# w_out with tokens on the partitions, norms by rows, and u of the next round loaded in the middle of a round

## The chip, the cores and the metric

The kernel runs on one core of a Trainium2 chip. The time is the device time of one execution in microseconds (us). Engines: PE multiplies matrices, ACT (scalar), DVE (vector) and POOL do elementwise work, SP issues most DMAs. All five take their instructions in order.

## The reference

One layer of a hybrid decoder over 1024 prompt tokens and 8 x 4 decode tokens (1056 rows, width 1024). The stages up to the merged gates stay as they are; the change is in what follows them:

```python
def rmsnorm(x, g):
    r = lax.rsqrt(jnp.mean(xf * xf, axis=-1, keepdims=True) + RMS_EPS)
    return (xf * r).astype(x.dtype) * g
...
y = (jax.nn.sigmoid(ga) * ya + jax.nn.sigmoid(gb) * yb) @ w_out      # 1024 -> 1024
x = x + gt_m * rmsnorm(y, g_post_mix)
h2 = rmsnorm(x, g_pre_mlp) * (1 + sc_f) + sh_f
u = jnp.square(jax.nn.relu(h2 @ w_up))                               # 1024 -> 4096
x = x + gt_f * rmsnorm(u @ w_down, g_post_mlp)                       # 4096 -> 1024
```

`gt_m`, `sc_f`, `sh_f`, `gt_f` are vectors of 1024 that depend on the sequence (one for the prompt, eight for the decode rows). All is float32.

## The kernel before

**Precision.** A float32 product is three fp32r matmuls per block of 128 rows of the contraction: with each operand split into a rounded part h and the remainder l, they are h·h, h·l and l·h. So each operand needs a cast (ACT) and a difference (DVE or POOL). For weights this is `split4` (L1234 to L1241): a cast of 128x512 (L1238) and a difference (L1240) that goes to POOL, and every third time to DVE.

**Stages.** Times are from the span's start. `merge_b` (L1197) ends at 1011; its result m, split, lies in R0 to R7, channels on the partitions, in four chunks of 264 tokens.

1. *w_out* (1017 to 1129). Weights stationary, m moving: for each of 8 blocks of 128 output channels and each chunk 24 matmuls of 264 columns (L1458 to L1460), tokens in two halves of 528 one after the other: 768 matmuls. y comes out with channels on the partitions, as the residual x must then lie: 80 transposes turn x (L1334).
2. *Norms* (`norms`, L1352). With channels on the partitions, a sum over channels is a matmul by ones (L1266), and 1/rms is spread over the partitions by another (L1279). Between them stand scalings (L1344), adds (L1366), squares and sums (L1371, L1372), one block of 528 columns at a time.
3. *Operands* (`operands`, L1393). Strassen's scheme for `w_up` works on 2x2 blocks of h2 and of the weights: seven products instead of eight. The sums of blocks of h2 (L1405 to L1408) are split as well (L1312, L1313).
4. *plain* (1129 to 1220). While half 1 still goes through norms and operands, the first six column pairs of `w_up` are multiplied with half 0 by the ordinary scheme: 576 matmuls of 264 columns (L1513 to L1515).
5. *pair* (L1520; 1220 to 1505). Ten column pairs with both halves and the six with half 1 alone, by Strassen: 2184 matmuls of 264 columns (L1489 to L1491). The weights' block sums S (L1530 to L1533) and the results' adds (L1547) are on DVE. u goes to memory (L1502).
6. *Down* (1495 to 1913). Eight rounds of 512 rows of `w_down`, each 288 matmuls of 352 columns (L409 to L411). `load_u` (L1585) brings u of a round back and splits it: four casts (L1594), four differences (L1595) in turn on POOL and DVE. For round 0 it is called after two of the six half pairs and writes R0 to R3; for the others it is called at the round's start. The last round ends chunk by chunk with the norm, the residual and the output; x is turned back for it (L1658).

**What sets the order.** A scheduler places the instructions of each engine from the program's order and its own cost model; `tc.issue_after(ins)` and the tables `AT_OUT`, `XT_AT` and `AT_UP` say after which matmul a step of norms and operands is issued. Tiles have names and fixed numbers of buffers: a tile waits until the last reader of the buffer is done. DMAs of the queue SP are issued in order, and one that waits for a buffer holds back those behind it.

## Time and profile before

| | us |
|---|---|
| three runs | 1918.61, 1920.29 (median), 1930.76 |
| the profiled execution | 1914.69 |
| its span, first to last instruction | 1913.0 |
| PE busy | 1839.1 (96%) |
| DVE / ACT / POOL busy | 960.2 (50%) / 829.5 (43%) / 542.2 (28%) |
| mean granted clock | 0.976 of 2.4 GHz |

A matmul's busy time begins before the one ahead of it has ended, so a PE that is busy all the time need not be at its peak; the distance from one start to the next is what a matmul costs. The rows on which the prediction rests stand in a section below.

### The profile page before, as it was taken

What the parts mean: (1) busy time and instruction counts of PE and PEld (TensorE: products, weight loads), DVE (VectorE), ACT (ScalarE), POOL (GpSimd) and SP (SyncE); (2) the same over time, 40 slices, a digit from 0 to 9 for tenths busy, and PEclk for the clock granted to TensorE, in tenths of its full rate; (3) what the DMA queues carried; (4) which work ended last, traced back from release to release, by engine and by line L of the source; (5) the groups of instructions that cost most, each with busy time, mean ns of one, the idle gap of its engine ahead of it and who ended that gap; (6) DMA issues with size and microseconds to landing.
All of it is one profiled execution on the core that took longest, in us unless ns stands there. A gap on an engine that the chain in (4) does not pass through costs nothing.

```text
span 1913.0 us, 31223 instructions
## 1 busy us (share of the span) xinstructions
PE 1839.1 (96%) x12425; PEld 1733.9 (91%) x12425; DVE 960.2 (50%) x1904; ACT 829.5 (43%) x1513; POOL 542.2 (28%) x461
## 2 busy tenths in 40 slices
...
GB/s 272 78 69 60 148 92 68 56 79 111 174 168 220 70 62 58 77 201 111 67 97 156 123 99 161 94 107 119 90 134 148 122 135 90 90 90 90 90 55 128
DMA packets 180874, 213.29 MB, mean 111 GB/s; under 512 B 13940, under 2 KB 142512, under 8 KB 180728
## 3 DMA queue, kind: packets, MB, share of 16 engines
...
## 4 chain that ended last, share of the span: by engine, by line
PE 86%; DVE 5%; DMA 4%; issue 1%; ACT 1%; SPq 1%; POOL 1%; DVEq 0%; ACTq 0%; POOLq 0%
PE ps_g L409 17%; PE ps_g L411 17%; PE ps_g L410 17%; PE ps_s L685 2%; PE ps_g L1489 2%; PE ps_g L1491 2%; PE ps_g L1490 2%; PE ps_t L710 2%; PE ps_s L682 1%; PE ps_s L1491 1%; PE ps_s L1489 1%; PE ps_s L1490 1%; PE ps_t L1489 1%; PE ps_t L1490 1%; PE ps_t L1491 1%
## 5 line engine op out<-in xcount | busy, mean ns | idle before, releaser
L409 PE MATMUL ps_g<-Xh,wh 128*128 128x352 f32 (+1 forms) x1176 | 393.3, 335 | 0.2 <-ACT Xh L351 0.2
L411 PE MATMUL ps_g<-Xh,wl 128*128 128x352 f32 (+1 forms) x1176 | 389.6, 333 | 0.0
L410 PE MATMUL ps_g<-Xl,wh 128*128 128x352 f32 (+1 forms) x1080 | 355.9, 330 | 1.1 <-DVE Xl L352 0.9
L1240 POOL TENSOR_TENSOR pl<-raw,ph 128x512 fp32r<-128x512 f32 x116 | 170.4, 1473 | 304.4 <-ACT ph L1238 286.3
L409 PEld LDWEIGHTS ps_g<-Xh,wh 128*128 128x128 f32 (+1 forms) x1176 | 222.6, 189 | 6.0 <-issue 3.0
L411 PEld LDWEIGHTS ps_g<-Xh,wl 128*128 128x128 f32 (+1 forms) x1176 | 221.5, 189 | 5.9 <-issue 4.4
L1238 ACT CAST ph<-raw 128x512 fp32r<-128x512 f32 x160 | 98.2, 619 | 266.7 <-PE ps_g L410 186.1
L410 PEld LDWEIGHTS ps_g<-Xl,wh 128*128 128x128 f32 (+1 forms) x1080 | 203.4, 188 | 7.2 <-issue 3.9
L271 POOL TENSOR_TENSOR wl<-wr,wh 128x1024 fp32r<-128x1024 f32 x26 | 63.0, 2424 | 434.6 <-ACT wh L270 376.1
L1626 DVE TENSOR_TENSOR acc<-acc,ps_g 128x352 f32<-128x352 f32 x144 | 74.1, 519 | 156.5 <-PE ps_g L411 156.5
L409 PE MATMUL ps_g<-uhb,ph 128*128 128x352 f32 x288 | 93.8, 328 | 2.6 <-ACT uhb L1594 1.9
L410 PE MATMUL ps_g<-ulb,ph 128*128 128x352 f32 x288 | 94.2, 327 | 1.7 <-POOL ulb L1595 1.7
L411 PE MATMUL ps_g<-uhb,pl 128*128 128x352 f32 x288 | 94.4, 328 | 0.0
L409 PE MATMUL ps_g<-uha,ph 128*128 128x352 f32 x288 | 93.5, 325 | 0.0
L411 PE MATMUL ps_g<-uha,pl 128*128 128x352 f32 x288 | 93.3, 324 | 0.0
L410 PE MATMUL ps_g<-ula,ph 128*128 128x352 f32 x288 | 93.0, 323 | 0.0
L270 ACT CAST wh<-wr 128x1024 fp32r<-128x1024 f32 x52 | 54.4, 1047 | 73.2 <-PE ps_g L410 54.6
L1240 POOL TENSOR_TENSOR pl<-S,ph 128x512 fp32r<-128x512 f32 x42 | 56.8, 1355 | 102.3 <-ACT ph L1238 101.2
L686 DVE CUSTOM_DVE_ANT_0 Pt<-ps_s,nF 128x384 f32<-128x384 f32 (+4 forms) x96 | 51.8, 554 | 64.0 <-PE ps_t L710 39.5
L693 ACT ACTIVATE Pt<-Pt,nm 128x128 f32<-128x128 f32 (+3 forms) x64 | 49.7, 777 | 31.8 <-DVE nm L691 20.7
L712 ACT CAST PT<-ps_t 128x512 fp32r<-128x512 f32 (+1 forms) x80 | 40.5, 545 | 52.9 <-PE ps_t L710 52.1
L1240 DVE TENSOR_TENSOR pl<-raw,ph 128x512 fp32r<-128x512 f32 x44 | 34.2, 778 | 58.0 <-ACT ph L1238 55.9
...
## 6 DMA issues: line engine op xcount, KB each, us to landing
...
raw<-in_w_up SPq DMA_DIRECT2D x22, 1024.0 KB, 5.9
...
raw<-in_w_down SPq DMA_DIRECT2D x16, 1024.0 KB, 4.9
...
raw<-in_w_out SPq DMA_DIRECT2D x8, 1024.0 KB, 5.5
```

What stands on the lines that cost most here:

```text
L270: act.copy(wh, wr)
L271: (dve if lo_turn[0] % 2 else pool).tensor_sub(wl, wr, f(wh))
L409: pe.matmul(o, wh[:, k], rh(k, a, b), start=(k == 0), stop=False)
L410: pe.matmul(o, wh[:, k], rl(k, a, b), start=False, stop=False)
L411: last = pe.matmul(o, wl[:, k], rh(k, a, b), start=False, stop=(k == nk - 1))
L686: dve.tensor_tensor_reduce(Pt[:, k0:k1], s_, nF[:, k0:k1], 1.0, -3.0e38, ALU.add, ALU.max, mx[:, pi:pi + 1])
L1238: act.copy(h_, src)
L1240: (dve if turn[0] % every == 0 else pool).tensor_sub(l_, src, f(h_))
L1489: pe.matmul(o, wh[:, k], xh[:, k], start=first and k == 0, stop=False, skip_group_check=True)
L1490: pe.matmul(o, wh[:, k], xl[:, k], start=False, stop=False, skip_group_check=True)
L1491: pe.matmul(o, wl[:, k], xh[:, k], start=False, stop=k == 3, skip_group_check=True)
L1626: dve.tensor_tensor(accs[a // 352](ft), accs[a // 352](ft), o, ALU.add)
```

## The change

- `merge_b` now has chunks of 256, 256, 256 and 288 tokens; the last 32 are the decode rows, which are also kept in float32 (`md`). The last two blocks of `w_pb` are split into other slots. `gt_m` is made ahead of it, turned by 8 transposes, and written to memory (`d_gt`).
- w_out is turned round: 128 tokens of m are stationary and half the columns of w_out (512) move. Eight tiles of tokens by two column halves by 24: 384 matmuls of 512 columns. `w_half` splits one column half as eight pieces of 128x512. The decode rows (tile 8) are 16 float32 matmuls with 32 columns of the array each, plus two that sum the four partial results.
- The norms work by rows: ACT squares with a sum along the row, POOL makes 1/rms of 128x1 (L1402), DVE scales and adds (L1414 to L1420); x is loaded as it lies. `gt_m` comes as rows broadcast to all partitions (18 DMAs, L1341 and L1344). Only h2 is turned to channels on the partitions (72 transposes, L1434 to L1446).
- The halves are 512 and 544 tokens. The six plain column pairs become five pairs by Strassen with half 0 alone (420 matmuls of 256 columns), in which the last two turns and half 1's operands are issued. Then come eleven full pairs and five with half 1 alone (272 columns). In the five, `split4` gives every second difference to DVE; in plain nearly all (every=99) went to POOL.
- `load_u` uses R0 to R3 for round 0 and R4 to R7 for round 1, and is called for the next round in the middle of a round; all its differences are on DVE.
- x after the first norm is stored by rows, so the last round loads it as it lies: the 48 transposes L1658 are gone, and no chunk uses `finish_cm` any more. The row buffers alternate between `ula` and `uha`.

```diff
 CH = ((0, 352), (352, 704), (704, 1056))
-TQ = 264
-CQ = tuple((a, a + TQ) for a in range(0, T, TQ))
-PRE = 6
-TH = T // 2
-AT_OUT = (1, 1, 2, 1, 2, 1, 1, 0, 1, 2, 2, 2, 2, 1, 1, 1)
-XT_AT = (3, 4, 5, 6, 7)
-AT_UP = ((3, 1), (2, 2), *((0, n) for n in (1, 1, 2, 1, 2, 1, 0, 1, 1, 2, 1, 2, 2, 1, 1, 1, 1, 1, 0, 0, 0, 0)))
+CQ = ((0, 256), (256, 512), (512, 768), (768, T))
+PRE = 5
+AT_OUT = (((), (), ("d",), (), ()), ((), (), ("d",), (0,), (1,)), ((2, "D"), (3,), ("o",), (8, "o")),
+          (("o",), ("o", "o"), (4, "o"), (5, "o")))
+AT_UP = (0, 0, 1, 0, 0, 1, 1, 1, 1, 1, 1, 1, 1, 1)
 NPC = 6
 NW = 3
 TCARGS = {"schedule_with_timeline_sim": True}
...
+    MG = [tuple(xs(f"R{2 * q + i}", [P, 8, 256]) for i in range(2)) for q in range(4)]
+    md = tl(mgp, [P, 8, ND], F32, "RD", 1)
...
+    d_gt = tl(dr, [9, D], F32, "d_gt")
+    gt_r = slot("VB", [9, D])
+    for q in range(2):
+        pt = bank("t")
+        for k in range(4):
+            pe.transpose(pt[:9, k * P:(k + 1) * P], gt_m[:, 4 * q + k], ident)
+        act.copy(gt_r[:, q * 512:(q + 1) * 512], pt[:9])
+    sp.dma_start(d_gt, gt_r)
...
-            sgs[a] = tl(yp, [P, TQ], F32, "sg", 6)
+            sgs[a] = tl(yp, [P, 288], F32, "sg", 5)[:, 0:b - a]
...
-            mh, ml = MG[a // TQ]
...
+            mh, ml = MG[a // 256]
+            act.copy(mh[:, ft], sg[:, 0:256])
+            dve.tensor_sub(ml[:, ft], sg[:, 0:256], f(mh[:, ft]))
+            if b == T:
+                act.copy(md[:, ft], sg[:, 256:])
 
...
+        elif ft == 6:
+            w2 = slot("QA", [P, 4, 2 * P], F32R), slot("VA", [P, 4, 2 * P], F32R)
+            wr = tl(wp, [P, 4, 2 * P], F32, "wr", NW)
+            sp.dma_start(wr, w_pb[:, ft * P:(ft + 2) * P].rearrange("(k p) c -> p k c", p=P))
+            act.copy(w2[0], wr)
+            dve.tensor_sub(w2[1], wr, f(w2[0]))
...
+    def w_half(c):
+
+        out = []
+        for kh in range(2):
+            wr = raw_w(w_out, 4 * kh, 4, c * 512, 512)
+            for k in range(4):
+                pl = (w2p, "ph", "pl", NPC) if len(out) < 6 else (xo, "xh", "xl", 2)
+                h_ = tl(pl[0], [P, 512], F32R, pl[1], pl[3])
+                l_ = tl(pl[0], [P, 512], F32R, pl[2], pl[3])
+                act.copy(h_, wr[:, k])
+                (pool if k % 2 else dve).tensor_sub(l_, wr[:, k], f(h_))
+                out.append((h_, l_, wr[:, k]))
+        return out
...
+        sp.dma_start(gtb[c], d_gt[0:1, col].broadcast_to([P, 512]))
+        gtd.append(tl(w2p, [P, 4, P], F32, "S", 4).rearrange("p a b -> p (a b)"))
+        for b in range(NB):
+            sp.dma_start(gtd[c][b * TD:(b + 1) * TD], d_gt[1 + b:2 + b, col].broadcast_to([TD, 512]))
...
+                mh, ml = MG[self.t // 2]
+                c = slice(self.t % 2 * P, self.t % 2 * P + P)
+                o = bank8("gsgsg")
+                for k in range(8):
+                    pe.matmul(o, mh[:, k, c], W[k][0], start=(k == 0), stop=False)
+                    pe.matmul(o, mh[:, k, c], W[k][1], start=False, stop=False)
+                    last = pe.matmul(o, ml[:, k, c], W[k][0], start=False, stop=(k == 7))
+                return o, last.ins
...
+            acc = bank("o")
+            for k in range(8):
+                j = k % 4
+                last = pe.matmul(acc[32 * j:32 * j + 32], md[:, k], W[k][2], start=(k < 4), stop=(k >= 4))
+            if not self.part:
+                self.t3 = tl(xo, [P, D], F32, "t3", 1)
+            self.msb = self.t3[:, 0:512]
+            act.copy(self.msb, acc)
+            return None, last.ins
...
+        def summed(self):
+            o = bank("o")
+            pe.matmul(o[:ND], sum4d, self.msb, start=True, stop=True)
+            return o
...
+        def second(self, o):
+
+            n, c0, c1 = self.n, self.c0, 1 - self.c0
+            col = lambda c: slice(c * 512, c * 512 + 512)
+            t, x = self.tt[:n], self.x[:n]
+            self.square(t[:, col(c1)], o[:n], "b")
+            ss = tl(xo, [P, 1], F32, "qc", 3)
+            dve.tensor_tensor(ss[:n], self.part["a"][:n], self.part["b"][:n], ALU.add)
+            rr = self.rstd(ss, "1")
+            dve.scalar_tensor_tensor(t[:, col(c1)], o[:n], rr[:n], self.g[c1][:n], ALU.mult, ALU.mult)
+            dve.scalar_tensor_tensor(t[:, col(c0)], self.y0[:n], rr[:n], self.g[c0][:n], ALU.mult, ALU.mult)
+            dve.tensor_tensor(x, x, t, ALU.add)
+            sp.dma_start(d_x1[self.t0:self.t0 + n], x)
+            self.square(t, x, "d")
+            r2 = self.rstd(self.part["d"], "2")
+            dve.tensor_scalar(t, x, r2[:n], None, ALU.mult)
...
+            for q in range(2):
+                pt = bank("t").rearrange("p (a b) -> p a b", b=P)
+                for k in range(4):
+                    pe.transpose(pt[:, k], self.tt[:, (4 * q + k) * P:(4 * q + k + 1) * P], ident)
+                for k in range(4):
+                    y, ft = Q[h][q][:, k, a:a + P], 4 * q + k
+                    if k % 2:
+                        dve.tensor_scalar(y, pt[:, k], a_f[:, ft, 0:1], sh_f[:, ft, 0:1], ALU.mult, ALU.add)
+                    else:
+                        act.activation(y, pt[:, k], AF.Identity, bias=sh_f[:, ft, 0:1], scale=a_f[:, ft, 0:1])
...
         if th == 0:
-            part(th, "B12", B12, at["B12"])
-            part(th, "B22", B22, at["B22"])
-            yield
-        t3 = tl(qp if at["t3"][0] == "L" else mgp, [P, 2, 4, TQ], F32, at["t3"], 1)[:, 0]
+            t3 = tl(xo, [P, D], F32, "t3", 1).rearrange("p (a b) -> p a b", b=HQ[0])
+        else:
...
+    AT = ({"y": ("L0", "L1"), "B11": "R0", "B21": "R1", "T2": "R2", "T1": "R3", "T3": "L0", "T4": "R4", "B22": "R5"},
+          {"y": ("L2", "L3"), "B11": "R6", "B21": "R7", "T2": "L1", "T1": "M0", "T3": "L2", "T4": "M1", "B22": "M2"})
...
+    for n_, (c, ts) in enumerate(((0, (0, 8, 1, 2, 3)), (1, (0, 8, 1, 2, 3)), (1, (4, 5, 6, 7)), (0, (4, 5, 6, 7)))):
+        if c not in W:
+            W = {c: w_half(c)}
...
     def pair(i, hs):
+        every = 3 if len(hs) == 2 else 2
...
+    def tail_tasks():
+        for t in (6, 7):
+            rows[t].turn()
+            yield
+        yield from operands(1)
+        yield
...
     for i in range(PRE):
-        plain(i, anchors)
-    for _ in chain:
+        pair(i, (0,))
...
-            if n_ == 0:
-                t = tl(mgp, [P, 2, T], F32R, f"R{i}", 1)
+            if n_ < 2:
+                t = xs(f"R{4 * n_ + i}", [P, 2, T])
                 ht, lt = t[:, 0], t[:, 1]
...
-            (dve if i % 2 else pool).tensor_sub(lt, f(lt), f(ht))
+            dve.tensor_sub(lt, f(lt), f(ht))
...
-        if j == 1:
+        if j == 2:
...
+            if q and j + 1 < NJ and j != 1:
+                us[j + 1] = load_u(j + 1)
...
+    def residual(c):
+
         yts = []
-        for t0, t1 in tok_tiles(a, b):
-            yt = tl(dnp, [P, T], F32, "ula", FC)[:, :D]
-            for q in range(2):
-                pt = bank("s")
-                for k in range(4):
-                    pe.transpose(pt[:t1 - t0, k * P:(k + 1) * P], x1(q * 4 + k)[:, t0 - a:t1 - a], ident)
-                act.copy(yt[:t1 - t0, q * 512:(q + 1) * 512], pt[:t1 - t0])
+        for t0, t1 in tok_tiles(*CH[c]):
+            yt = tl(dnp, [P, T], F32, ("ula", "uha")[c % 2], FC)[:, :D]
+            sp.dma_start(yt[:t1 - t0], d_x1[t0:t1])
```

The scheduler moves instructions beyond this. Three places follow. SP, from the last loads of merge_b (`sg`) to the first two loads of w_out (`raw`). Before:

```order
L1201 DMA sg_10272<-d_sg_571 128x264
L1201 DMA sg_10274<-d_sg_571 128x264
L1201 DMA sg_10276<-d_sg_571 128x264
L1231 DMA raw_10369<-in_w_out 128x8x256
L1231 DMA raw_10499<-in_w_out 128x8x256
```

Now:

```order
L1223 DMA sg_10300<-d_sg_571 128x256
L1223 DMA sg_10302<-d_sg_571 128x288
L1341 DMA S_10395<-d_gt_9718 128x512
L1344 DMA S_10397<-d_gt_9718 4x512 x8
L1341 DMA S_10406<-d_gt_9718 128x512
L1344 DMA S_10408<-d_gt_9718 4x512 x8
L1257 DMA raw_10421<-in_w_out 128x4x512
L1257 DMA raw_10439<-in_w_out 128x4x512
```

Eighteen DMAs now stand between the last `sg` and the first `raw`. The `raw` loads wait for matmuls of merge_b's sixth block, no longer for the end of merge_b.

DVE, in the norms of the last tokens, while PE is in the plain pairs. Before (L and ssq hold y, x and the sums; no difference of a weight stands here):

```order
L1366 TENSOR_TENSOR L_2024_10984<-L_2024_10984,R_2125_11672 128x528
L1344 SCALAR_TENSOR_TENSOR L_2024_10984<-L_2024_10984,mod_23_174,n_11840 128x496 x3
L1366 TENSOR_TENSOR L_2023_10983<-L_2023_10983,R_2124_11671 128x528
L1372 TENSOR_TENSOR ssq_11850<-ssq_11850,n_11887 128x528
L1366 TENSOR_TENSOR L_2024_10984<-L_2024_10984,R_2125_11672 128x528
L1372 TENSOR_TENSOR ssq_11850<-ssq_11850,n_11934 128x528
```

Now, in the norms of tiles 4 to 7 (M holds x and y by rows, S gt_m or a block sum of weights, pl a weight's l part):

```order
L1266 TENSOR_TENSOR pl_11364<-raw_11331,ph_11363 128x512
L1401 TENSOR_SCALAR v_2095_11133<-qd_11131 128x1
L1416 TENSOR_TENSOR M_2098_11141<-M_2098_11141 128x1024
L1401 TENSOR_SCALAR v_2113_11224<-qc_11222 128x1
L1266 TENSOR_TENSOR pl_11418<-S_11333,ph_11417 128x512
L1420 TENSOR_SCALAR M_2088_11092<-M_2088_11092,r_2096_11134 128x1024
L1552 TENSOR_TENSOR S_11335<-raw_11331 128x512
L1414 SCALAR_TENSOR_TENSOR M_2109_11193<-ps_g_11195,r_2114_11225,S_10395 128x512
L1415 SCALAR_TENSOR_TENSOR M_2109_11193<-y_2061_10999,r_2114_11225,S_10406 128x512
```

The weights' differences (L1266) and block sums (L1552) of the first pairs now stand between norms on DVE; PE needs each `pl` for its next product.

ACT, at the end of round 0 and the start of round 1 of the down stage. Before:

```order
L1624 COPY acc_2778_15966<-ps_g_16312 128x352
L1238 CAST ph_16600<-raw_16552 128x512
L1624 COPY acc_2779_15967<-ps_g_16326 128x352
L1594 CAST uhb_16346<-ulb_16347 128x1056
L1594 CAST uhb_16351<-ulb_16352 128x1056
L1594 CAST uhb_16356<-ulb_16357 128x1056
L1594 CAST uhb_16361<-ulb_16362 128x1056
```

Now round 1's u is in R4 to R7, and its last two casts stand among the half pairs (L1264 casts weights, L1563 and L1584 read results):

```order
L1620 CAST R_2830_15737<-R_2830_15737 128x1056
L1264 CAST ph_15496<-raw_15393 128x512
L1563 COPY v_15351<-ps_s_15263 128x272
L1563 COPY v_15422<-ps_t_15405 128x272
L1264 CAST ph_15515<-S_15398 128x512
L1620 CAST R_2831_15741<-R_2831_15741 128x1056
L1264 CAST ph_15545<-raw_15543 128x512
```

Round 1's casts stood behind the last copy of round 0's results; they now stand ahead of round 0's first copies.

## Rows read from the trace of the kernel before

**Rows 1.** The page, part 1: busy us of each engine (share) xinstructions.

```profile
PE 1839.1 (96%) x12425; PEld 1733.9 (91%) x12425; DVE 960.2 (50%) x1904; ACT 829.5 (43%) x1513; POOL 542.2 (28%) x461
```

**Rows 2.** PE in five stretches: us, busy us (xmatmuls), granted clock, DMA.

```profile
1220.00:1240.00 20.00, 17.39 (x132) 0.91 0.24 81
1240.00:1430.00 190.00, 190.00 (x1562) 1.00 0.35 111
1430.00:1460.00 30.00, 25.17 (x179) 0.89 0.44 143
1550.00:1570.00 20.00, 15.77 (x81) 0.83 0.34 109
1590.00:1830.00 240.00, 240.00 (x1485) 1.00 0.26 90
```

**Rows 3.** Lines of PE: duration ns min/median/max, first to last start us.

```profile
L1458 PE MATMUL ps_g<-R,ph x152: 278/283/588, 1017.1 to 1126.0; 128*128 128x264 f32 x152
...
L1515 PE MATMUL ps_g<-R,pl x92: 278/284/422, 1129.7 to 1220.4; 128*128 128x264 f32 x92
...
L1491 PE MATMUL ps_t<-L,pl x76: 278/286/293, 1245.4 to 1505.0; 128*128 128x264 f32 x76
...
L409 PE MATMUL ps_g<-uhb,ph x288: 318/323/495, 1552.4 to 1790.2; 128*128 128x352 f32 x144
...
L409 PE MATMUL ps_g<-R,ph x96: 321/323/495, 1494.8 to 1549.8; 128*128 128x352 f32 x96
...
L411 PE MATMUL ps_g<-uhb,dl x96: 318/325/410, 1837.6 to 1893.0; 128*128 128x352 f32 x96
```

**Rows 4.** Timeline of PE: start us, us, engine, line, operation.

```profile
446.86 0.39 PE L682 MATMUL ps_s<-KA,QA 128*128 128x512 f32 x1
447.09 0.23 PE L684 MATMUL ps_s<-u,u 128*128 128x128 bf16 x1
...
1042.02 1.04 PE L1334 MATMUL ps_t<-u,S 128*128 128x128 f32 x8
1042.81 0.37 PE L1458 MATMUL ps_g<-R,ph 128*128 128x264 f32 x1
```

**Rows 5.** A line of queue SP: duration ns min/median/max, starts us.

```profile
L1201 SPq DMA_DIRECT2D sg<-d_sg x32: 319/320/505, 964.3 to 1004.9; - x32
```

**Rows 6.** The page, part 6: DMAs, KB each, us to landing.

```profile
raw<-in_w_out SPq DMA_DIRECT2D x8, 1024.0 KB, 5.5
```

**Rows 7.** Groups of DVE, 1220 to 1505: busy us, mean ns | idle.

```profile
L1500 DVE SCALAR_TENSOR_TENSOR n<-n 128x528 f32<-128x528 f32 x25 | 25.6, 1025 | 17.4 <-ACT n L1564 17.4
L1240 DVE TENSOR_TENSOR pl<-S,ph 128x512 fp32r<-128x512 f32 x22 | 16.7, 759 | 34.2 <-ACT ph L1238 34.2
L1531 DVE TENSOR_TENSOR S<-S,raw 128x512 f32<-128x512 f32 x15 | 13.6, 905 | 7.5 <-POOL pl L1240 7.5
...
L1240 DVE TENSOR_TENSOR pl<-raw,ph 128x512 fp32r<-128x512 f32 x17 | 11.7, 685 | 11.0 <-ACT ph L1238 9.1 <-POOL pl L1240 1.9
...
L1547 DVE TENSOR_TENSOR n<-ps_g,v 128x264 f32<-128x264 f32 x26 | 11.0, 425 | 14.2 <-ACT v L1543 11.1 <-PE ps_g L1491 3.1
```

**Rows 8.** The same view of DVE, 1017 to 1225.

```profile
L1344 DVE SCALAR_TENSOR_TENSOR L<-L,mod,n 128x528 f32<-128x528 f32 (+1 forms) x32 | 35.3, 1160 | 10.3 <-ACT n L1280 10.3
```

**Rows 9.** Lines of DVE and POOL: duration ns min/median/max, starts us.

```profile
L1240 POOL TENSOR_TENSOR pl<-raw,ph x116: 1258/1292/3753, 1017.1 to 1803.1; 128x512 fp32r<-128x512 f32 x116
...
L1240 DVE TENSOR_TENSOR pl<-raw,ph x44: 676/691/2522, 1018.1 to 1791.3; 128x512 fp32r<-128x512 f32 x44
...
L1313 DVE TENSOR_TENSOR R<-L,R x8: 1245/1520/2743, 1128.2 to 1232.0; 128x1056 fp32r<-128x1056 f32 x8
```

**Rows 10.** Two stretches: us, busy us of PE, PEld, DVE, ACT, POOL, clock.

```profile
1129.00:1220.00 91.00, 84.42 (x656) 83.14 (x655) 61.13 (x57) 51.50 (x100) 62.74 (x37) 0.94 0.41 132
1220.00:1505.00 285.00, 277.56 (x2226) 276.42 (x2224) 140.75 (x210) 137.73 (x280) 108.68 (x78) 0.98 0.36 117
```

**Rows 11.** A line of the last round: duration ns min/median/max, starts us.

```profile
L1693 DVE SCALAR_TENSOR_TENSOR ula<-ps_t,rt,ula x8: 742/750/751, 1898.8 to 1906.1; 128x512 f32<-128x512 f32 x6, 96x512 f32<-96x512 f32 x2
```

More of the change, by code (lines that the diff above doesn't have):

```diff
@@ L1389, in blocks @@
[L1389 to L1391 removed]
     def operands(th):
[L1395 removed]
+        B11, B12, B21, B22 = [Q[th][k][:, :, c * HQ[th]:(c + 1) * HQ[th]] for k in range(2) for c in range(2)]
         at = AT[th]
@@ L1479, in hybrid_kernel @@
+    for _ in ops0:
+        pass
+    xos.close()
+    nps = ExitStack()
+    npl = nps.enter_context(tc.tile_pool(name="np", bufs=1, reuse_waits="tile"))
     _mark(nc, "up")
```

360 lines of the change are left out of this document (133 added, 227 removed).

## The prediction

> **What bounds the kernel now.** The page's first part shows PE busy for 96% of the span [rows 1], but a busy PE may be waiting inside its pipeline, so I read on by counting matmuls. In a stretch without stalls, 1562 matmuls of 264 columns start in 190 us, one per 0.1216 us, and 1485 of 352 columns in 240 us, one per 0.1616 us [rows 2]. That is 0.455 ns per further column: 0.118 us for 256, 0.125 for 272, 0.234 for 512 columns; a 512-column matmul of an earlier stage has 0.23 to the next start [rows 4], and I take 0.232. Eight transposes take 0.79 us and delay the next matmul a little: 0.11 each [rows 4].
>
> Next the starts of single lines give the stages [rows 3]: w_out and the plain pairs 1017.1 to 1220.5 (203.4 us), pairs and round 0 to the end of R's matmuls at 1550.3 (329.8), rounds 1 to 6 to 1837.4 (287.1), the last round and its tail to 1913 (75.6). Count times pitch against these shows where PE loses:
> - w_out and plain hold 768 + 576 matmuls, 163.4 us of 203.4. The 40 us between are transposes, sums by matmul, waits and half clock: this is the largest loss.
> - Pairs and round 0 hold 2184 x 0.1216 + 288 x 0.1616 = 312 us of 329.8, 18 lost. Of these 4 lie in 1220 to 1240 (132 matmuls where 164 fit) and 8 in 1430 to 1460 (179 where 247 fit, clock 0.89), where u of round 0 is loaded [rows 2].
> - Rounds 1 to 6 hold 279.2 of 287.1; 7 of the 8 lost lie in 1550 to 1570 (81 where 124 fit) [rows 2].
>
> So PE sets the time, with stalls at joints. POOL is busy in 69% of the plain stretch and 38% of the pairs, DVE in 67% and 49% [rows 10].
>
> **The change part by part.** The sum is made against the profiled execution, 1914.7 us with a span of 1913.0; the median of the three runs is 5.6 above it.
>
> *Start of w_out: +2 us (0 to +4).* The raw loads no longer wait for the end of merge_b, but SP now has 18 DMAs ahead of them. An `sg` load occupies SP for 0.32 us, and the last one goes out at 1004.9 [rows 5]. With one buffer less it goes about one chunk (12 matmuls, 1.5 us) later, and 8 added transposes cost 0.9: 1007.3. Then 18 x 0.32 = 5.8 us, an issue of 0.5, landing 5.5 us later [rows 6] and a cast of 0.6: first matmul at 1019.5, against 1017.1. Were the small DMAs free, the gain would be 4; so w_out starts about where it did.
>
> *w_out and the pairs with half 0: 175 us (160 to 193) in place of 203.4.* For PE alone: 384 x 0.232 = 89.1; 16 decode matmuls and two sums, whose form no row shows, between 0.12 each as a matmul of 264 columns and four times that (2 to 9 us), taken at 0.23 as 512 columns, 4; 56 transposes 6.2; half clock at the start 2; then 420 x 0.118 = 49.6 and 16 transposes 1.8. That is 152.7 us, 51 less than now: fewer matmuls (half 0 of the sixth pair moves to the next term), no sums and spreads by matmul, no waits.
>
> But DVE decides. It runs in order, and from the group with tiles 4 to 7's second halves on (PE reaches it at 77 us), norms of four tiles, both halves' operands and the differences and block sums of five pairs' weights stand in one queue; the order of DVE above shows a piece `pl` between two norms. Before, the plain pairs' pieces were POOL's. From there to the first full pair I count on DVE: 40 of 512 columns with two SBUF inputs (17 weight differences, 23 block sums), 0.68 us at least [rows 9]; 4 scalings of the stored half of y, 0.75 as L1693 [rows 11]; 4 products of u with itself, taken at 0.69; 18 of 1024 to 1088 columns (operands) and 4 adds of x, taken at 1.25 as L1313's least [rows 9]. That is 27.2 + 3 + 2.8 + 22.5 + 5 = 60.5 us, all with two SBUF inputs, at the least prices. The others (12 adds at 0.425 [rows 7], 4 scalings from PSUM at 0.75 as L1693 [rows 11], 4 scalings of 1024 by a scalar, taken at 1.1 between 0.75 and 1.245, 16 turns at 0.3 and small ones) are 20.
>
> What do the 60.5 cost beside POOL? In the pairs, where POOL is busy 38%, four such groups took 67.6 us for 79 instructions [rows 7], 1.26 times 0.68. In the plain stretch, with POOL at 69% [rows 10], and in w_out L1344 took 1.160 on the mean [rows 8] where L1693, the same operation from PSUM, takes 0.75 [rows 11]: 1.55 times. The changed stretch gives POOL 18 weight differences at 1.29 [rows 9], one block difference (about 2.7) and 8 roots (about 0.9): 33 us of some 95, 35%. That is nearest to the pairs, so 1.26: 76 + 20 = 96 us. DVE can begin at 79 (77, and the wait for POOL's difference of blocks); 79 + 96 = 175. At the least prices it is 160, at 1.55 it is 193. So PE waits about 22 us in the first pairs, and these waits are what is late next.
>
> *Eleven full pairs, five half pairs, round 0: 331 us (327 to 337) in place of 329.8.* 924 x (0.118 + 0.125) + 420 x 0.125 = 277.2, and 46.5 for round 0: 323.7, 11.7 more than before, since half 0 of a sixth pair moved here. The 4 us at 1220 are in the term above. The load of u at 1430 finds R0 to R3 free earlier, but its casts still stand among the weights' casts on ACT and wait for a DMA that waits for a product: 3 of the 8 us stay, 4 of the other losses too.
>
> *Rounds 1 to 6: 280 (279 to 287) in place of 287.1.* Round 1's casts were behind the last copy of round 0 and now come before round 0's first; the 7 us go. That the later rounds load in mid-round brings nothing: they ran at full pitch.
>
> *Last round: 66 (63 to 70) in place of 75.6.* 48 transposes go (5.3 us). In the tail DVE made 12 scalings of 0.75 from 1898.8 on [rows 11], since all tiles shared `ula`; with alternating buffers six remain, 4.5 less.
>
> Sum: 1017.1 + 2 + 175 + 331 + 280 + 66 = 1871 us of span; with the 1.7 between span and execution **1873 us**, 42 below the profiled execution.
>
> **The rule weighed.** DVE and POOL slow each other in these rows: a difference of 512 columns on DVE has 0.691 in the middle and 2.522 at most, on POOL 1.292 and 3.753 [rows 9]. The Trainium skill (SBUF — State Buffer, section "SBUF: two separate sides") says that a DVE instruction with two SBUF inputs and a POOL instruction that reads SBUF lock each other out for the whole instruction. By that rule the two add up, and the sum would be that of the second rival below. The rows of the pairs show less than that, since a wait counts only where both have work at once.
>
> **The rivals.** A change of less than 1% (1901 to 1939 around the median) I count as no change.
> 1. *DVE runs at its least prices* (POOL happens to wait elsewhere): 160 in place of 175, 1858 us. For it: the weight differences of raw tiles in the pairs took 0.685 on the mean [rows 7]. Chance 0.20.
> 2. *DVE and POOL exclude each other fully in the stretch*: 60.5 + 20 + 33 = 113.5 us, ending at 192; 1890 us. For it: L1344 at 1.55 times; against: the pairs at 1.26. Chance 0.17.
> 3. *Slower: DVE and PE take turns.* The adds L1547 of a pair stand in DVE's queue ahead of the next pairs' pieces and wait for PE's products, which wait for the pieces before. If nothing of PE's remaining 75.5 us overlaps DVE's 96, the stretch ends at 79 + 96 + 75.5 = 250: 1948 us. It passes the old median when 47 of the 75 us don't overlap. For it: the queue is in order; against: the same adds stand so in the pairs now, and 1240 to 1430 runs without a gap [rows 2]. Chance 0.05.
> 4. *The earlier loads don't come earlier*: round 1's casts hold up weights' casts or R is freed late, the tail keeps its length. 7 + 8 + 9 give back up to 24: 1880 to 1897. Chance 0.08.
>
> My forecast has 0.50. The range 1846 to 1905 takes in rivals 1, 2 and 4, the start's and the last round's bounds and, above, the 5.6 us by which the median stood over the profile; outside lie rival 3 and the corners where all ends meet. Faster by over 1% are the forecast, rival 1 and nearly all of rival 2: 0.86; within 1% the upper ends of 2 and 4 and half measures of 3: 0.09; slower 0.05.
>
> **What would show it.** Right: first matmul of w_out at about 1019; 512-column matmuls 0.23 apart; gaps of PE in the first five pairs, each ended by a DVE `pl`, some 22 us in all, with DVE busy over 90% there; no gap at the start of round 1; about six scalings after the last matmul. Wrong: PE gaps in w_out itself at the change of the column half (pieces of the weights late), which I priced at nothing since a piece freed by the last tile has the 5.6 us of that tile to be split; low clock through the first pairs; or PE waiting for ACT there, which has casts and squares for both.

## The result, and the profile after

The change made the kernel faster by a little less than half of what I forecast: the changed kernel has a median of 1899.21 us (1891.69 to 1910.08, 14 runs), the kernel before, run beside it, 1918.70 (1910.51 to 1930.76, 14 runs). The ratio is 0.9896 [0.9870, 0.9923], 19.5 us less; I had forecast 42 less, 1873, with a range of 1846 to 1905.

The profiled execution of the changed kernel took 1903.87 us, with a span of 1902.1. Up to the end of `merge_b` it was 10 us later than that of before, although both programs have nearly the same work there (last section). So all stages are measured from the end of `merge_b` on: 1021.8 here, 1011.2 before. From there to the end are 901.8 us before and 880.3 now, 21.5 less, which agrees with the medians.

The page's first part answers to [rows 1]:

```profile
PE 1824.4 (96%) x11871; PEld 1688.0 (89%) x11871; DVE 979.4 (51%) x2001; ACT 814.9 (43%) x1502; POOL 415.2 (22%) x387
```

PE's share is the same as before, so again only counts of matmuls show where it loses. Five stretches of the changed kernel, in the columns us, busy us of PE, PEld, DVE, ACT, POOL (x instructions), PE's granted clock, share of DMA, GB/s; they answer to [rows 2, 10]:

```profile
1220.00:1420.00 200.00, 200.00 (x1634) 200.00 (x1633) 81.56 (x141) 86.86 (x184) 58.18 (x45) 1.00 0.36 109
1425.00:1475.00 50.00, 45.85 (x357) 44.53 (x356) 35.24 (x48) 29.80 (x58) 18.43 (x13) 1.00 0.60 193
1475.00:1510.00 35.00, 31.68 (x236) 30.96 (x235) 18.73 (x24) 20.85 (x40) 15.42 (x13) 1.00 0.52 178
1590.00:1600.00 10.00, 7.67 (x46) 7.10 (x45) 4.20 (x6) 3.01 (x4) 1.27 (x1) 1.00 0.65 236
...
1136.50:1216.50 80.00, 61.94 (x475) 59.09 (x474) 75.05 (x103) 48.15 (x97) 37.63 (x26) 0.94 0.37 118
```

The full pairs run without a gap, 1634 matmuls in 200 us, 0.1224 apart. The second to fourth row are losses that I had forecast as gone or small: 85 us at the end of the pairs hold 593 matmuls, and at 1590, the start of round 2, 46 start in 10 us where 62 fit at 0.1616. The last row is the first pairs, with DVE busy 94% of the time, as forecast. PE's gaps there are not the ones that I forecast (some 22 us, each ended by a DVE `pl`). Its waits in the same 80 us, in the columns instruction, releaser, us in total, times, longest:

```profile
PE ps_t L1440 <- DVE L L1444: 7.1, 1, 7.1
PE ps_g L1527 <- ACT v L1563: 3.6, 3, 2.2
PE ps_o L1527 <- ACT v L1563: 3.1, 1, 3.1
...
PE ps_t L1529 <- DVE pl L1266: 0.8, 1, 0.8
PE ps_g L1529 <- DVE pl L1266: 0.8, 1, 0.8
```

They add up to 18.0 us. The longest is a turn (L1440) that waits until DVE has scaled results of an earlier turn (L1444). ACT ends 8.5 us (6.7 by copies of results, 1.8 by casts of weights), `pl` only 1.6.

Lines of PE, in the columns of [rows 3], give the bounds of the stages:

```profile
L1361 PE MATMUL ps_s<-ph,R x42: 391/397/797, 1031.5 to 1134.4; 128*128 128x512 f32 x42
L1369 PE MATMUL ps_o<-raw,RD x32: 592/617/1063, 1029.7 to 1068.7; 128*32 128x512 f32 x32
L1527 PE MATMUL ps_g<-R,ph x208: 276/282/386, 1136.5 to 1464.1; 128*128 128x256 f32 x87, 128*128 128x272 f32 x17
L406 PE MATMUL ps_g<-R,ph x192: 321/323/433, 1495.7 to 1596.1; 128*128 128x352 f32 x192
L406 PE MATMUL ps_g<-uhb,dh x96: 318/325/412, 1834.7 to 1887.4; 128*128 128x352 f32 x96
```

| stage, us | before | forecast | measured |
|---|---|---|---|
| end of `merge_b` to the first matmul of w_out | 5.9 | 7 | 7.8 |
| w_out, and the first pairs to their 420th matmul (106.9 + 77.4) | 203.4 | 175 | 184.3 |
| the other pairs and round 0 | 329.8 | 331 | 335.9 |
| rounds 1 to 6 | 287.1 | 280 | 284.9 |
| last round and tail | 75.6 | 66 | 67.4 |
| sum | 901.8 | 859 | 880.3 |

The forecast of 7 is 5.9 and the 2 us forecast, less 0.9 for the eight transposes, which lie ahead of the end of `merge_b`. Three terms carry 19 of the 21 us that are missing: the second, third and fourth rows. PE's waits at the end of the pairs and at the start of round 2, in the same columns:

```profile
PE ps_s L1527 <- ACT v L1563: 2.2, 2, 1.2
PE ps_g L1529 <- DVE pl L1266: 1.4, 2, 1.1
PE ps_g L406 <- DVE n L1567: 1.4, 1, 1.4
...
PE ps_g L406 <- ACT uha L1620: 1.6, 1, 1.6
```

The first three are from 1425 to 1515, each short and ended by ACT or DVE; the fourth is at round 2's start. The start of round 1, at 1549.9, has no wait, as forecast. What ACT and DVE themselves waited for from 1425 to 1515 is longer:

```profile
ACT R L1620 <- DMA R<-d_u: 10.0, 6, 4.8
```

```profile
DVE R L1621 <- ACT R L1620: 9.6, 4, 5.5
```

L1620 and L1621 are the cast and the difference of u in `load_u`. They stand among the last pairs' copies and pieces of weights, and the whole queue stands behind them until the load has landed. Round 2's u is issued by SP only behind two raw loads (start us, us, instruction):

```profile
1563.62 23.73 SPq L1257 DMA_DIRECT2D raw<-in_w_down  x2
1587.45 9.13 SPq L1619 DMA_DIRECT2D ula<-d_u  x4
```

### The profile page after: what moved, and what is told of

It reads as the page before. It is cut to its first block, busy times and chain, and to the rows that moved or that the text cites. A ratio compares the mean times of both kernels' runs of the same rounds, so it can differ in the third digit from the quotient of the medians.

```text
span 1902.1 us, 30069 instructions
## 1 busy us (share of the span) xinstructions
PE 1824.4 (96%) x11871; PEld 1688.0 (89%) x11871; DVE 979.4 (51%) x2001; ACT 814.9 (43%) x1502; POOL 415.2 (22%) x387
## 4 chain that ended last, share of the span: by engine, by line
PE 84%; DMA 6%; DVE 5%; issue 2%; ACT 1%; POOL 1%; SPq 0%; POOLq 0%; DVEq 0%; ACTq 0%
PE ps_g L406 17%; PE ps_g L408 17%; PE ps_g L407 17%; PE ps_s L682 2%; PE ps_g L1529 2%; PE ps_g L1527 2%; PE ps_g L1528 2%; PE ps_t L707 2%; PE ps_t L1529 1%; PE ps_t L1527 1%; PE ps_t L1528 1%; PE ps_s L1527 1%; PE ps_s L1528 1%; PE ps_s L1529 1%; PE ps_s L679 1%
## 5 line engine op out<-in xcount | busy, mean ns | idle before, releaser
L1266 POOL TENSOR_TENSOR pl<-raw,ph 128x512 fp32r<-128x512 f32 x74 | 101.8, 1377 | 338.4 <-ACT ph L1264 338.4
L1264 ACT CAST ph<-raw 128x512 fp32r<-128x512 f32 x119 | 73.5, 619 | 224.1 <-PE ps_g L407 189.6
L1266 POOL TENSOR_TENSOR pl<-S,ph 128x512 fp32r<-128x512 f32 x51 | 70.7, 1387 | 143.0 <-ACT ph L1264 126.9
L1264 ACT CAST ph<-S 128x512 fp32r<-128x512 f32 x84 | 51.5, 617 | 58.9 <-PE ps_g L1528 16.6
L406 PE MATMUL ps_g<-R,ph 128*128 128x352 f32 x192 | 62.3, 324 | 2.3 <-DVE n L1567 1.4
L710 DVE TENSOR_TENSOR PT<-ps_t,PT 128x512 fp32r<-128x512 f32 (+1 forms) x80 | 48.3, 631 | 28.4 <-ACT PT L709 28.2
L1527 PE MATMUL ps_g<-R,ph 128*128 128x256 f32 (+1 forms) x208 | 59.0, 284 | 4.1 <-ACT v L1563 3.1
```

Source lines behind the costliest of these rows:

```text
L406: pe.matmul(o, wh[:, k], rh(k, a, b), start=(k == 0), stop=False)
L1264: act.copy(h_, src)
L1266: (dve if turn[0] % every == 0 else pool).tensor_sub(l_, src, f(h_))
L1527: pe.matmul(o, wh[:, k], xh[:, k], start=first and k == 0, stop=False, skip_group_check=True)
```

## The experiments

All experiments change the changed kernel. Their stages, each from one profile, counted as above; "480th" is the start of the 480th matmul of the pairs after the first one (PE alone would need 58 us and 3 for transposes), and the stage behind it ends with round 0's first matmul:

| us | start | w_out | to 480th | to round 0 | rounds 0 to 2 | rest | sum |
|---|---|---|---|---|---|---|---|
| changed kernel | 7.8 | 106.9 | 84.7 | 274.5 | 152.5 | 254.0 | 880.3 |
| e_usplit | 7.9 | 106.9 | 84.7 | **268.2** | 153.4 | 253.6 | 874.8 |
| e_round_start | 7.9 | 107.1 | 87.8 | **270.2** | 153.3 | 253.9 | 880.1 |
| e_ring | 7.8 | 106.2 | 87.0 | 277.1 | **147.5** | 254.2 | 879.8 |
| e_gt_late | **1.5** | **102.8** | 87.5 | 276.6 | 152.4 | 253.9 | 874.6 |
| e_dec | 9.0 | **103.2** | 87.7 | 275.6 | 152.4 | 253.9 | 881.7 |
| e_ula | 8.0 | 106.0 | 86.2 | 275.7 | 152.4 | **254.0** | 882.3 |
| e_pool | 7.7 | 106.2 | **95.5** | 273.9 | 152.3 | 254.7 | 890.1 |
| e_dvepl | 7.7 | 106.3 | **79.4** | 276.8 | 152.0 | 254.8 | 876.9 |
| e_nopl | 7.5 | 106.4 | **73.0** | 274.9 | 150.9 | 254.7 | 867.3 |
| e_lessdve | 7.6 | 107.0 | **85.6** | 274.9 | 152.0 | 254.8 | 881.7 |
| e_combo | 2.6 | 101.0 | 87.9 | 268.6 | 148.4 | 255.0 | 863.6 |
| e_best | 2.6 | 102.3 | 82.8 | 268.5 | 148.5 | 255.5 | 860.2 |

Stages that an edit leaves alone show the spread of this measure: 84.7 to 87.9 to the 480th, 273.9 to 277.1 to round 0, 106.0 to 107.1 in w_out, 150.9 to 152.5 in rounds 0 to 2. e_round_start, e_ula and the four edits of the first pairs were run once each, so for them only stages count.

**u cast later (e_usplit).** The loads of u stay where they are; round 0's casts and differences are put behind named copies and sums of the last half pairs on ACT and DVE, round 1's behind the last of them.

```diff
 # in load_u
-            act.copy(ht, f(lt))
-            dve.tensor_sub(lt, f(lt), f(ht))
+            if n_: cast_u(ht, lt)
 # round 0's: called from pair, behind its first and second sum
+        with after(la[0]): act.copy(ht, f(lt))               # la: the last copy v
+        with after(ld[0]): dve.tensor_sub(lt, f(lt), f(ht))  # ld: the last sum on DVE
```

> Changed kernel, but the casts and differences of u of rounds 0 and 1 are made to stand behind copies of the last half pairs in ACT's and DVE's order; their loads stay where they are. Theory (the 10 to 12 us that PE loses between 1425 and 1510 come from casts of u that wait for a load in ACT's and DVE's order, with the pieces of the weights and the copies behind them): from 1425 on, the 593 matmuls of the two stretches need 6 to 10 us less, no wait of ACT or DVE for R<-d_u over 2 us stands among the pairs, and the whole is 6 to 10 us shorter (about 1891 in the median). Rival A (the stall is the change of tiles in the half pairs, too few matmuls behind each weight piece): the same stretches take the same time within 2 us. Rival B (the wait only moves): round 0 starts late, PE waits for uha/R there for 4 us or more, gain below 3.

The stage became 6.3 us shorter than in the changed kernel, and 5.7 to 8.9 shorter than where it is left alone; the median is 1893.37, ratio 0.9866 [0.9803, 0.9929]. The first half of the stretch now holds 404 matmuls in 50 us instead of 357:

```profile
1412.00:1462.00 50.00, 50.00 (x404) 50.00 (x404) 30.43 (x47) 27.46 (x56) 18.40 (x14) 1.00 0.61 193
1462.00:1497.00 35.00, 31.82 (x235) 30.70 (x234) 24.57 (x28) 25.93 (x47) 17.37 (x11) 1.00 0.52 172
```

The second row holds 352-column matmuls of round 0 too, so its count is lower without a stall. Round 0 lost only 0.9: the theory holds in the stage. The median alone would not show it, since its interval overlaps that of the changed kernel. The edit moves the casts of both rounds; the next run tells them apart.

**u at the rounds' starts (e_round_start).** This undoes the mid-round load and keeps the rest.

```diff
-            if n_ < 2:
+            if n_ < 1:
...
-        if j == 2:
+        if j == 1:
...
-            if q and j + 1 < NJ and j != 1:
-                us[j + 1] = load_u(j + 1)
```

> Changed kernel, but u of every round after the first is loaded at that round's start, into the tiles uh and ul, as in the kernel before. Theory (the mid-round load is what took away the gap between rounds 0 and 1): from the first matmul of round 0 to that of round 1 or from round 1 to round 2, together 102.6 us in the changed kernel, now 105 to 110, with PE waiting for uha or ula at round 1's start for 5 to 7 us; in the changed kernel the same wait stood at round 2's start with 1.8 to 3 us. Rounds 3 to 7 as before, 46.7 us each. Rival (the gap had gone because R4 to R7 were free early, and loading time does not matter): no gap at round 1.

A gap comes back at round 1: rounds 0 and 1 take 106.7 us in place of 102.6, as expected, though PE waits only 2.4 us for uhb and ulb, half of what I expected or less. Round 2's gap goes (46.6 us in place of 49.9): 153.3 us against 152.5 for the three rounds. What I had not expected is the stage ahead of round 0, 270.2 us, 4 to 7 less than in the others. Without the early load of round 1, none of its casts stands in ACT's and DVE's order among the pairs. So the mid-round load, as the change made it, gave back at round 1 about what it cost at round 2, and cost 4 us or more ahead of round 0: most of e_usplit's 6.3.

**u always mid-round (e_ring).**

```diff
-            if n_ < 2:
-                t = xs(f"R{4 * n_ + i}", [P, 2, T])
...
+            t = xs(f"R{4 * (n_ % 2) + i}", [P, 2, T])
+            ht, lt = t[:, 0], t[:, 1]
...
-            if q and j + 1 < NJ and j != 1:
+            if q and j + 1 < NJ:
```

The last round's rows of x, for which `uha` and `ula` served, move into the same tiles (not shown).

> Changed kernel, but u of all rounds alternates between the same two sets of four tiles, and every round's u is loaded in the middle of the round before (round 2's too, which the changed kernel loads at its start). Theory (the 4 to 5 us lost at 1590 to 1600 are round 2's load, issued only when round 1's raw weights have gone out): no gap of PE over 0.5 us at the start of round 2, rounds 1 to 6 take 280 to 282 us in place of 285.7, the whole is 4 to 5 us shorter. Rival A (u tiles come free too late in a ring of two, so that each round now waits): gaps of 1 us or more at several rounds, rounds 1 to 6 at 286 or longer.

Both joints are gone, with no wait of PE from 1540 to 1822; rounds 1 and 2 take 46.7 us each (48.5 and 49.9 in the changed kernel), and rounds 1 to 6 280.3, the term that I forecast. Median 1890.87, ratio 0.9868 [0.9803, 0.9934].

**Raw weights ahead of the gains (e_gt_late).**

```diff
+    W0 = w_half(0)
     sum4d = tl(xo, [P, ND], F32, "sd", 1)
...
-    W = {}
+    W = {0: W0}
```

> Changed kernel, but the two raw loads of w_out are issued ahead of the 18 small loads of the gains. Theory (SP's 18 small loads, 1017.3 to 1024.5, set the start): from the end of merge_b to the first matmul of w_out there are 1.5 to 3.5 us in place of 8.2, the whole is 5 to 7 us shorter. Rival A (the raw tiles' space comes free only with the last matmul of merge_b): 6 to 8 us stay. Rival B (DVE decides up to the full pairs): the start comes earlier, but the stretch from the first w_out matmul to the first full pair grows by as much, since DVE has its work later only by its own queue; gain below 2.

The start fell to 1.5 us, as expected, and w_out became 4.1 shorter too, which I had not foreseen. The wait of 8 us was followed by half clock (a granted 0.53 to 0.66, the lower level of 1.2 GHz for most of it), in the changed kernel until 1034.7. Stretches of the changed kernel, then of this one, in the columns of the stretches above:

```profile
1022.00:1030.00 8.00, 0.33 (x4) 0.23 (x8) 1.71 (x7) 1.01 (x4) 0.84 (x1) 0.66 0.65 226
1030.00:1035.00 5.00, 5.00 (x17) 2.75 (x10) 4.20 (x4) 3.92 (x8) 4.17 (x3) 0.53 1.05 409
1035.00:1045.00 10.00, 10.00 (x38) 5.40 (x37) 2.00 (x3) 1.31 (x3) 2.19 (x2) 1.00 0.35 122
```

```profile
1012.00:1020.00 8.00, 6.55 (x58) 6.00 (x56) 4.88 (x12) 2.57 (x9) 4.32 (x5) 1.00 0.80 265
1020.00:1030.00 10.00, 9.91 (x52) 6.77 (x44) 6.81 (x9) 4.35 (x9) 6.78 (x4) 1.00 0.45 148
```

With a wait of 1.5 us the clock stays at its upper level. But the clock is not all of the 4.1 us: the scheduler also grouped the decode rows' matmuls otherwise. Those of the first column half, in the changed kernel and then in this one (start, us, x records; two records are one matmul):

```profile
1029.67 1.94 PE L1369 MATMUL ps_o<-raw,RD 128*32 128x512 f32 x8 [7.82 <-DMA raw<-in_w_out]
...
1038.31 1.05 PE L1369 MATMUL ps_o<-raw,RD 128*32 128x512 f32 x2
...
1040.88 1.04 PE L1369 MATMUL ps_o<-raw,RD 128*32 128x512 f32 x2
...
1043.91 1.05 PE L1369 MATMUL ps_o<-raw,RD 128*32 128x512 f32 x4
```

```profile
1019.50 1.06 PE L1370 MATMUL ps_o<-raw,RD 128*32 128x512 f32 x8 [1.45 <-DMA raw<-in_w_out]
...
1029.52 1.07 PE L1370 MATMUL ps_o<-raw,RD 128*32 128x512 f32 x8
```

Two groups fewer, at 0.98 us each (next experiment), are 2.0 of the 4.1. So 18 small loads ahead of a large one cost 6.3 us of waiting and some 2 of half clock. The next stages took some back, within their spread; from the end of `merge_b` to the end 5.7 us are left; median 1894.59, ratio 0.9868 [0.9796, 0.9940].

**Decode rows in fours (e_dec).**

```diff
-            o, last = R.gemm(W[c])
+            with (after(last) if t == 8 else nullcontext()): o, last = R.gemm(W[c])
```

> Changed kernel, but the eight matmuls of the decode rows stand together behind the last matmul of a prompt tile, in two fours, in place of pieces of four, one, one, two and one, four, three. Theory (a group of one to four column groups costs PE 1.0 us at full clock, whatever their number, so the seven groups and two sums cost 10 us where I took 4): four groups and two sums remain, some 6 us, and w_out (first to last matmul) takes 102.5 to 104 us in place of 106.7. Rival A (the price goes by matmul, 0.25 to 0.5 each): w_out stays at 106 to 107. Rival B (the raw tile is held longer, so that the other column half's weights come late): PE waits for ph or pl in w_out, 107 or more.

w_out fell by 3.7 us to 103.2, although it began at half clock here too: the theory. The start grew by 1.2, since the first decode matmuls had filled part of the wait for the first cast. The timeline of the changed kernel, then of this one (a matmul of L1369 leaves two records):

```profile
1060.66 0.40 PE L1363 MATMUL ps_g<-ph,R 128*128 128x512 f32 x1
1060.99 1.04 PE L1369 MATMUL ps_o<-raw,RD 128*32 128x512 f32 x2
1061.97 0.49 PE L1361 MATMUL ps_g<-ph,R 128*128 128x512 f32 x1
1062.39 1.06 PE L1369 MATMUL ps_o<-raw,RD 128*32 128x512 f32 x8
1063.39 0.50 PE L1362 MATMUL ps_g<-pl,R 128*128 128x512 f32 x1
```

```profile
1032.34 0.40 PE L1363 MATMUL ps_s<-xh,R 128*128 128x512 f32 x1
1032.67 1.92 PE L1369 MATMUL ps_o<-raw,RD 128*32 128x512 f32 x16
1034.52 0.50 PE L1362 MATMUL ps_g<-pl,R 128*128 128x512 f32 x1
```

One matmul alone (x2) keeps PE from the next for 0.98 us, four on four column groups (x8) for 1.00, eight for 1.85. The Trainium skill (TensorE: Matmul & The Clock Gate, section "Part 3: Packing small matmuls — row/col tiling") says that matmuls with outputs in different column groups run at the same time; the rows agree, and show the other side of it: a group that is broken up by the scheduler pays the full price for each part. The total did not move (1901.19, ratio 0.9912 [0.9878, 0.9947]). In the profile the first pairs took 3.0 us more and the start 1.2; whether the first pairs take back what w_out gains is asked below.

**One tile name in the last round (e_ula).**

```diff
-            yt = tl(dnp, [P, T], F32, ("ula", "uha")[c % 2], FC)[:, :D]
+            yt = tl(dnp, [P, T], F32, "ula", FC)[:, :D]
```

> Changed kernel, but all row tiles of the last round go through the tile ula. Theory (alternating row tiles took DVE's scalings out of the tail): from the last matmul of the last round to the end of the span 17 to 19 us in place of 14.4. Rival (the tail is set by the last chunk's own transposes, scalings and stores): 14.4 within 1.

The rival: 14.4 us behind the last matmul, to the tenth. The scalings of the changed kernel, which answer to [rows 11], then of this one:

```profile
L1710 DVE SCALAR_TENSOR_TENSOR ula<-ps_t,rt,ula x8: 740/746/752, 1857.1 to 1894.0; 128x512 f32<-128x512 f32 x6, 96x512 f32<-96x512 f32 x2
```

```profile
L1710 DVE SCALAR_TENSOR_TENSOR ula<-ps_t,rt,ula x14: 734/741/751, 1857.2 to 1894.1; 128x512 f32<-128x512 f32 x10, 96x512 f32<-96x512 f32 x4
```

Both begin at 1857, and six stand behind the last matmul, where all twelve of before began at 1898.8. So it was not the alternation. Before, the first third of the tokens was finished by columns (`finish_cm`), whose last transposes stood at 1894, and its copies held `ula` until 1898; the change does all thirds by rows. That this is what brought the scalings forward is read from the two traces and was not tried alone.

**The first pairs: who sets them (e_pool, e_dvepl, e_nopl, e_lessdve).** The first three change which engine makes the low pieces of the weights in the five pairs with half 0; the fourth takes other work off DVE.

```diff
-        every = 3 if len(hs) == 2 else 2
+        every = {(0,): 99, (1,): 2, (0, 1): 3}[hs]   # e_pool; e_dvepl: 1 for 99
...
+        if not every: return h_, h_                  # e_nopl (0 for 99), in split4
...
-            dve.tensor_tensor(x, x, t, ALU.add)      # e_lessdve, in Rows.second
```

> Changed kernel, but in the five first pairs (half 0 alone) all differences of the weights' pieces are POOL's; before, every second was DVE's (17 pieces). I read the time from the first matmul of these pairs to their 480th, which was 84.7 us in the changed kernel and 84.7, 84.7, 87.5, 87.0, 87.7 over all five programs so far that leave this stretch as it is; PE alone would need 58 plus 3 for transposes. Theory (DVE's queue sets this stretch): with 17 x 0.7 to 1.2 us less on DVE the mark comes at 68 to 76. Rival A (DVE and POOL exclude each other, so a piece costs DVE's time wherever it is made): 80 to 90. Rival B (POOL at 1.3 to 2.5 us a piece becomes the bound): PE's waits are ended by POOL pl, mark at 80 or later.

> Changed kernel, but in the five first pairs all differences of the weights' pieces are DVE's (before, every second was POOL's). Theory (DVE and POOL exclude each other while both read two tiles of SBUF, so that the stretch is set by the sum of both): a piece costs 0.69 us on DVE in place of 1.29 on POOL, 18 pieces give back 10 us, the 480th matmul of the pairs comes 74 to 80 us after their first, against 84.7 to 87.8 in the programs that leave this stretch as it is and 95.5 with all pieces on POOL. Rival A (DVE alone sets the stretch, POOL's share runs beside it): 18 x 0.69 to 1.0 us more on DVE, mark at 95 to 103. Rival B (neither: the chain of norm, transpose, turn and operand does): within 2 us of 86.

> Changed kernel with no differences of the weights' pieces in the five first pairs (35 of them are left out, and the high part stands in their place in the products, so part of the computation is left out); PE's and ACT's instructions are the same. Theory (DVE and POOL together set the stretch): 17 x 0.69 and 18 x 1.29 are 35 us of the two engines, more than the 24 to 27 us that PE loses here, so the mark of the 480th matmul falls to 62 to 72 us. Rival (the chain of norm, transpose, turn and operand, or ACT): 80 or more.

> Changed kernel without DVE's additions of the residual x to the normed rows (nine of 1024 columns), so part of the computation is left out, and nothing else on any engine. Theory (DVE's queue sets the first pairs): the 480th matmul of the pairs comes 4 to 9 us sooner after their first (76 to 81 against 84.7 to 87.7), since four to six of these additions stand behind the point where DVE becomes the bound, at 1.2 to 1.5 us each. Rival (the stretch is set by ACT, by clock or by latency of the chain norm, transpose, turn, operand): less than 2 us.

With all pieces on POOL the mark comes 8 to 11 us later, with all on DVE 5 to 8 sooner, without any 12 to 15 sooner. So e_pool's theory, by which DVE's queue alone sets the stretch, is refuted (95.5 where it had 68 to 76); its rival A had the direction but too little of it, and B's sign is weak: POOL's `pl` ends 2.4 of the 21.9 us that PE waits in the first 80. e_dvepl came as expected; e_nopl, at 73.0, missed its 62 to 72 by little. DVE's operations with two inputs in SBUF tell why: groups of 80 us in e_pool, then in e_dvepl (busy us, mean ns | idle):

```profile
L1552 DVE TENSOR_TENSOR S<-raw 128x512 f32<-128x512 f32 x6 | 8.1, 1353 | 2.0 <-POOL pl L1266 2.0
...
L1452 DVE TENSOR_TENSOR M<-L,M 128x1088 fp32r<-128x1088 f32 x3 | 6.5, 2152 | 0.0
...
L1467 DVE TENSOR_TENSOR L<-L,L 128x1088 f32<-128x1088 f32 x1 | 2.3, 2262 | 0.0
```

```profile
L1266 DVE TENSOR_TENSOR pl<-S,ph 128x512 fp32r<-128x512 f32 x22 | 15.6, 718 | 1.5 <-ACT ph L1264 1.5
...
L1552 DVE TENSOR_TENSOR S<-raw 128x512 f32<-128x512 f32 x7 | 4.8, 679 | 0.0
L1452 DVE TENSOR_TENSOR M<-L,M 128x1088 fp32r<-128x1088 f32 x3 | 3.8, 1274 | 0.0
...
L1467 DVE TENSOR_TENSOR L<-L,L 128x1088 f32<-128x1088 f32 x1 | 1.3, 1277 | 0.0
```

The same block sum takes 0.679 us or 1.353, the same operand 1.274 or 2.152. This agrees with the Trainium skill (SBUF — State Buffer, section "SBUF: two separate sides"), by which such an instruction and one of POOL that reads SBUF block each other for the whole instruction. A piece given to POOL thus can cost DVE up to the time that POOL takes for it, 1.29 us in [rows 9], against 0.69 on DVE itself. e_lessdve is the miss: nine additions fewer on DVE, and the mark is at 85.6, the rival. It is a weak test, since in the changed kernel only three of the nine reach into these 80 us (4.7 us), and it speaks against the sum of DVE and POOL as much as against DVE alone. Its gain of 2.8 us at the 48th matmul was lost again behind the next wait for ACT. So not every us of DVE's queue counts here, as PE's waits say too, of which ACT ends nearly half. Which of the chain of norm, transpose, turn and operand holds PE there stays open, as do the 12 us that e_nopl still loses beyond PE's 61 (8.5 of them are waits, 5.2 for ACT's copies and 3.3 for DVE's norm).

**All edits together (e_combo, e_best).** The edits of e_usplit, e_gt_late, e_ring and e_dec; e_best has that of e_dvepl too.

> Changed kernel with four of the edits at once: u of rounds 0 and 1 cast behind the last half pairs' copies, raw loads of w_out ahead of the gains' loads, u of all rounds alternating in two sets of tiles and loaded mid-round, decode rows' matmuls in fours. Theory (the four losses are separate): from the end of merge_b to the end of the span 880.3 less 6 (u), 10 (start and the half clock behind it), 5 (round 2), 3.7 (decode), so 855 to 860, the median at 1874 to 1881. Rival (the first pairs take back what comes before them, since DVE and POOL set when they end): 863 to 870, 1882 to 1890.

> The kernel with the four edits, and in addition all differences of the first five pairs' pieces on DVE. Theory (DVE and POOL exclude each other): another 6 to 10 us less, 846 to 853 us from the end of merge_b, median 1865 to 1874. Rival (DVE alone): 8 to 15 us more than the four edits without it.

e_combo took 863.6 us from the end of `merge_b`, the lower end of the rival's, with a median of 1878.45 in the theory's range, ratio 0.9838 [0.9808, 0.9868]. Of u's edits 5.9 and 4.1 us stand in the table. Start and w_out gave 11.1: apart their two edits gave 10.4 and 2.5, but 2.0 of the first were decode groups, which the second removes as well. The first pairs were at their long end, 3 us back.

That may not be chance: in the three programs with a shorter w_out and these pairs unchanged the mark is at 87.5 to 87.9, in the five that change neither at 84.7 to 87.8, and e_best, which also has e_dvepl's edit, is at 82.8 where e_dvepl alone is at 79.4. So the first pairs may take back some 2 to 3 us of what w_out gains; no run separates that from the spread.

e_best: 860.2 us, median 1875.55, ratio 0.9800 [0.9774, 0.9826], 36 us less than the kernel before beside it (1911.55); its interval lies below that of the changed kernel. It missed its range of 846 to 853, with 3.4 us less than e_combo where I expected 6 to 10. Whether it is faster than e_combo the times don't tell.

## Why the prediction was right in its sign and wrong in its size

The sign came true, and half of the 42 us did not. Three steps of the sum failed: the decode rows' matmuls at 4 us (9.7 measured); round 1's casts, brought ahead of round 0 at no price (e_usplit gives back 6.3 for the casts of both rounds, where I had left 3); and "the 7 us go" between rounds 0 and 1, of which 4.9 came back at round 2. These are 14 of the 21 us. In the first pairs the time came near, by waits that were mostly not those forecast.

- **Start of w_out** (forecast 7 us from the end of `merge_b`): right, 7.8 (the prediction's items add up to 1019.7, not 1019.5). The half clock behind it, which no row of mine gave and which I took at 2 us, was about that by e_gt_late.
- **w_out** (forecast 101, measured 106.9): mis-sized at the decode rows. I took 0.23 us for each of 18 matmuls, 4 in all, with 9 as the upper end; the rows show 1.0 for each separate group at full clock, seven groups (the first at half clock, 1.87) and two sums, 9.7 in all. That is the whole miss of this stage, and e_dec gave 3.7 back by grouping alone.
- **First pairs** (forecast 74, PE's 51.4 and 22 of waiting): 77.4 to the 420th matmul, 26 over PE's, and DVE was busy 94% there. The size is luck in part. `pl` ended 1.6 of PE's 18.0 us of waits, where I had said all, and the waits for ACT, 8.5, are what I had named as a sign of being wrong. DVE and POOL do count most (12 to 15 us by e_nopl), and a piece costs more on POOL than on DVE (e_pool, e_dvepl), which is the exclusion that I had as a rival at 0.17. That rival's sum, 192 us from the start of w_out, was too long all the same: 184.3 measured, 178.6 without the decode rows' 5.7, against 175 in the forecast. Part of the queue's work is hidden, as e_lessdve shows.
- **Pairs and round 0** (forecast 331, measured 335.9): this step failed. I saw that the casts of u would wait in ACT's order, and let 3 of the old 8 us stay since the tiles come free earlier. But the loads still landed after the casts' turn, and round 1's casts, which I had brought forward at no price, had come to the same place: e_usplit shows 6.3. Without round 1's casts some 4 of them are gone (e_round_start), so the 3 us for round 0 alone were fair, and what I left out is what rival 4 has at 0.08: round 1's casts hold up the weights' casts. That all differences were DVE's now was not tried alone. The rest is that 256 columns are not proportionally cheaper than 264: full pairs run at 0.1224 where I had 0.1215, 1.7 us in 1848 matmuls.
- **Rounds 1 to 6** (forecast 280, measured 284.9): the step "the 7 us go" failed on its other half. Round 1's stall went, but as much as 4.9 us was lost at round 2. It was the first whose u is loaded only at the round's start, behind two raw loads in SP's queue. I had called the mid-round load of later rounds worth nothing because they ran at full pitch before; a round that changes tiles is not one of those. e_ring gave the 280.3.
- **Last round** (forecast 66, measured 67.4): right in size, by a wrong reason for the tail (e_ula).

Of the 21 us that were missing, e_combo gave back 16.7, and e_best 20.1.

## What to carry to other kernels

A load moved earlier also moves its cast earlier, into an in-order queue where everything behind it waits for the landing: move the load, and pin the cast behind work that is surely late enough. Where DVE with two SBUF inputs sets a stretch, handing work to POOL can lengthen it (95.5 us against 79.4 here). Price packed small matmuls by group as the scheduler leaves them, and follow a joint that you remove to the next place where tiles change.

## What the runs showed of the chip

The stretch behind 900 us, long before the change, varies between executions by ten us and more: PE falls to half clock and stays there for a time that differs. The same 40 us in the profile of before and in that of the changed kernel, where the programs are alike:

```profile
900.00:940.00 40.00, 40.00 (x214) 35.27 (x215) 17.86 (x62) 7.06 (x17) 6.62 (x6) 0.83 0.23 66
```

```profile
900.00:940.00 40.00, 40.00 (x161) 35.41 (x160) 11.34 (x44) 4.06 (x11) 5.06 (x5) 0.57 0.19 53
```

214 matmuls against 161, at a granted clock of 0.83 and 0.57; in the variants, which were not edited there, the clock of these 40 us lies between 0.57 and 0.96. The end of `merge_b` lay between 1004.3 and 1022.7 us in the thirteen profiles of the changed kernel and its variants, as wide as the spread of the changed kernel's times (1891.69 to 1910.08). That it makes most of that spread is inferred, since each kernel has one profile. A comparison of two single profiles must start behind it. Why PE falls to half clock there was not tried.
